# Norm and transpose chains of the output projections set beside the next product

## The chip, the cores and the metric

The kernel runs on one core of a Trainium2 chip. The metric is the device time of one execution in microseconds (us). In the tables PE is TensorE's matmul queue, PEld its weight loads, DVE is VectorE, ACT is ScalarE, POOL is GpSimd and SP is SyncE, which here only issues DMA transfers.

## The reference

One transformer-like block on x of 2048 rows by 1024 columns, in float32:

```python
h = rmsnorm(x, norm_mix_g)
q, k, v, u, vg = split(h @ w_in)                   # five parts of 512 columns
a_out = stick_breaking_attention(q, k, v)          # 8 heads of 64, causal
b_out = spatial_gating(gelu(u), gelu(vg), ...)     # 128-row blocks
mix = concat([rmsnorm(a_out, g[:512]), rmsnorm(b_out, g[512:])])
x = x + mix @ w_out                                # the output projection
h = rmsnorm(x, norm_mlp_g)
x = x + square(relu(h @ w_up)) @ w_down            # 4096 wide
return rmsnorm(x, norm_final_g)
```

## The kernel before, in words

The 2048 rows are worked in four chunks of 512 rows (c = 0 to 3), each of four blocks of 128 rows (tb = 0 to 3). Every float32 operand of a product is split in a high and a low half (`split`: ScalarE copies the high half, L85; VectorE subtracts to get the low half, L86), and each product is three matmuls (`mm3`, L93 to L95).

Attention is a generator, `side`, of 320 weighing steps and 7 more to drain. One step multiplies a query block with 512 keys (`z`, L370 and L371), takes two sigmoids (ScalarE, L377 and L379), a scan and a product (VectorE, L385 and L386), then, for an earlier step's result, four transposes (`tr`, L396), a split (`aT`, L85 and L86) and two matmuls into `av` (L414, L415). A head pair's result goes to DRAM as `a_d` (L426).

The rest of the block is made by other generators. `together(main, side, ratio)` runs `main` and after each of its yields adds `ratio` steps of `side` (0.5 for the output projections of chunks 0 and 1, 0.49 later). For chunks 0, 1 and 2 the order written out is:

1. a loop that runs `side` alone until the chunk's attention is drained;
2. `Out.operands` (5 yields): loads `st` (rows of `b_d`) and `at` (rows of `a_d`); for each tb the norm of `st`, four transposes and a split into `bm`; then the split of `at` into `am`, its squares and 16 column sums on TensorE (L524; 32 matmuls in the trace);
3. `Out.product` (32 yields): four groups, (half, part) = (0,1), (0,0), (1,1), (1,0). Part 1 multiplies `bm`, part 0 `am`. A group is four blocks of 12 matmuls, each added to `ys` on VectorE (L555). After the last group each block is written to `y_d` (L557);
4. `Out.turn` (8 yields): for each tb the norm of the row (squares on ScalarE, L574; `n_r` on GpSimd; scaling on VectorE, L576), and twice four transposes (L581) and a split into `hT`. Chunk 2 keeps no halves and copies `hT` on ScalarE, then writes it to `h_d` (L590).

After chunks 0 and 1 comes `up_plain` (256 yields): 16 rounds that load and split 256 columns of `w_up` (L618) and multiply them with `hT` of both chunks. After chunk 2 comes `down_plain` (256 yields): it loads `ys` of chunks 0 and 1 from `y_d` (L642), then for g = 0 to 7 loads and splits `left` (from `act_d`, L647) and `right` (from `w_down`, L654) and multiplies them, each block added to `ys` by L686.

All tiles of these stages named `t8` (8 KB in each partition) share one pool of 14 buffers; three PSUM banks named `mm` serve products and transposes alike. Tile gives each engine a fixed order of instructions when the program is built: the order of the code is the priority, and an instruction whose operands are not ready by its plan lets a later one go first. All loads and stores of these stages go out on SP's queue, in its fixed order.

Of the kernel before, what the change touches and what calls it, by code (L numbers as in the profile page):

```python
# [12 lines left out]
ALU = mybir.AluOpType  # L13
# [3 lines left out]
P = 128  # L17
D = 1024
# [5 lines left out]
TC = 512  # L24
NTB = TC // P
# [9 lines left out]
def block_kernel(ctx: ExitStack, tc: tile.TileContext, x, x_t, gmix, w_in, ln_g, ln_b, sgw, sgb,  # L35
                 outg, w_out, gmlp, w_up, w_down, gfin, out):
    nc = tc.nc
# [31 lines left out]
    a_d = dram.tile([SBW, T], F32, name="a_d")  # L69
# [262 lines left out]
    steps = [0]  # L332
# [6 lines left out]
    DRAIN = LATE + LAG  # L339
# [148 lines left out]
    class Out:  # L488


        def __init__(self, c, room):
            self.c, self.rm = c, room

        def operands(self):
            rm, c = self.rm, self.c
            self.rbs = []
            self.ready = [self.weights(0, 1)]
            st = rm.t8([4, SBW])
            nc.sync.dma_start(st, b_d[c * TC:(c + 1) * TC, :].rearrange("(n p) d -> p n d", p=P))
            at = rm.t8([4, TC])  # L500
            nc.sync.dma_start(at, a_d[:, c * TC:(c + 1) * TC].rearrange("(n p) t -> p n t", p=P))
            bm = self.bm = rm.pair([4, TC])
            for tb in range(NTB):
                sq = rm.t4([SBW], BF16)
                ssq = rm.small("rb_ssq")
                nc.scalar.activation(sq, st[:, tb, :], AF.Square, accum_out=ssq)
                m = rm.small("rb_m")
                nc.vector.tensor_scalar(m, ssq, 1.0 / SBW, EPS, ALU.mult, ALU.add)
                rb = rm.small("rb", bufs=2 * NTB)
                nc.gpsimd.tensor_tensor(rb, m, mhalf[:, 0:1], ALU.pow)  # L510
                self.rbs.append(rb)
                ps = rm.ps((P, 4, P))
                for e in range(4):
                    nc.tensor.transpose(ps[:, e, :], st[:, tb, e * P:(e + 1) * P], ident)
                ts_ = slice(tb * P, (tb + 1) * P)
                split(bm[0][:, :, ts_], bm[1][:, :, ts_], ps)
                yield
            am = self.am = rm.pair([4, TC])
            split4(am, at)
            nc.scalar.activation(at, at, AF.Square)  # L520
            pssq = rm.ps()
            for tb in range(NTB):
                for e in range(4):
                    nc.tensor.matmul(pssq[:, tb:tb + 1], at[:, e, tb * P:(tb + 1) * P], ones, start=e == 0, stop=e == 3)  # L524
            ra = rsqrt_mean(rm.pool, pssq[:, :NTB], NTB, SBW, "ra")
            self.ras = [ra[:, tb:tb + 1] for tb in range(NTB)]
            yield
# [4 lines left out]
                nc.sync.dma_start(w[i].bitcast(F32), wo_d[half, part, i])  # L532
            return w

        def product(self):
# [7 lines left out]
            ys = self.ys  # L543

            def group(half, part, m, rr):
                ws = self.ready.pop() if self.ready else self.weights(half, part)
                hs = slice(half * 512, (half + 1) * 512)
                for tb in range(NTB):
                    ts_ = slice(tb * P, (tb + 1) * P)
                    ps = rm.ps()  # L550
                    for e in range(4):
                        mm3(ps, m[0][:, e, ts_], m[1][:, e, ts_], ws[0][:, e, :], ws[1][:, e, :], e == 0, e == 3)
                        if e == 1:
                            yield
                    nc.vector.scalar_tensor_tensor(ys[tb][:, hs], ps, rr[tb], ys[tb][:, hs], ALU.mult, ALU.add)  # L555
                    if half == 1 and part == 0:
                        nc.sync.dma_start(y_d[c][:, tb, :], ys[tb])  # L557
                    yield

            yield from group(0, 1, self.bm, self.rbs)  # L560
            yield from group(0, 0, self.am, self.ras)
            yield from group(1, 1, self.bm, self.rbs)
            yield from group(1, 0, self.am, self.ras)

        def turn(self):

# [46 lines left out]
    def up_plain(hTs, rm):  # L613

        for q in range(16):
            acts = rm.t8([2, 2, TC])
            st = rm.t8([2, 8, P])
            nc.sync.dma_start(st, w_up[2 * q:2 * q + 2].rearrange("f p k c -> p f k c"))  # L618
            w = rm.pair([2, 8, P])
            for fi in range(2):  # L620
                split(w[0][:, fi], w[1][:, fi], st[:, fi])
            for fi in range(2):
                for i in range(2):
                    ps = rm.ps()
                    for k in range(KD):
                        h = hTs[i][k // 4]
                        mm3(ps, w[0][:, fi, k, :], w[1][:, fi, k, :], h[0][:, k % 4, :], h[1][:, k % 4, :],
                            k == 0, k == KD - 1)
                        if k % 2 == 1 and k < KD - 1:
                            yield  # L630
                    relu2(acts[:, i, fi, :], ps)
                    yield
            for i in range(2):
                nc.sync.dma_start(act_d[i][:, 2 * q:2 * q + 2, :], acts[:, i])

    def down_plain(rm, placed):

        ys = []
        for c in range(2):
            for t2 in range(2):  # L640
                y = rm.t8([2, D])
                nc.sync.dma_start(y, y_d[c][:, 2 * t2:2 * t2 + 2, :])  # L642
                ys += [y[:, 0, :], y[:, 1, :]]

        def left(c, g):
            st = rm.t8([4, TC])
# [12 lines left out]

        ND = 8  # L660
        c_now, n_now = 0, 0
        for g in range(ND):
            lefts, rights = {}, {}
            for turn in range(4):
                if turn == 2:
                    c_now = 1 - c_now
                elif turn > 0:
                    n_now = 1 - n_now
                c, n = c_now, n_now
                if c not in lefts:  # L670
                    lefts[c] = left(c, g)
                if n not in rights:
                    rights[n] = right(n, g)
                if g == ND - 1 and turn == 2:
                    placed.append(True)
                a, b = lefts[c], rights[n]
                ns = slice(n * 512, (n + 1) * 512)
                for tb in range(NTB):
                    ts_ = slice(tb * P, (tb + 1) * P)
                    ps = rm.ps()  # L680
                    for k in range(4):
                        mm3(ps, a[0][:, k, ts_], a[1][:, k, ts_], b[0][:, k, :], b[1][:, k, :], k == 0, k == 3)
                        if k == 1:
                            yield
                    y = ys[4 * c + tb]
                    nc.vector.tensor_tensor(y[:, ns], ps, y[:, ns], ALU.add)  # L686
                    if g == ND - 1 and turn % 2 == 1:
                        finish(rm, rm.t4([D], BF16), c, tb, y, nc.gpsimd)
                    yield
# [286 lines left out]
    def together(main, side=None, ratio=0.0):  # L976
# [3 lines left out]
        while True:  # L980
# [5 lines left out]
            while due >= 1.0:  # L986
                due -= 1.0
                if next(side, OPEN) is OPEN:
                    return OPEN

    base = ExitStack()
    sp = base.enter_context(tc.tile_pool(name="sp", bufs=1))
    mm_stack = ExitStack()
# [22 lines left out]
    with ExitStack() as es:  # L1016
# [22 lines left out]
        hTs = []  # L1039
        for c in range(2):  # L1040
            while steps[0] < 16 * (c + 1) * (c + 2) + DRAIN:
                next(side)
            o = Out(c, rm)
            together(o.operands(), side, R_O)
            together(o.product(), side, R_O)
            together(o.turn(), side, R_O)
            hTs.append(o.hT)
        together(up_plain(hTs, rm), side, R_U)
        while steps[0] < 16 * 3 * 4 + DRAIN:
            next(side)  # L1050
        o = Out(2, rm)
        together(o.operands(), side, R_U)
        together(o.product(), side, R_U)
        together(o.turn(), side, R_U)
        down = down_plain(rm, placed)
        assert together(down, side, R_U) is OPEN
    with tc.tile_pool(name="ext", bufs=1, side="right", reuse_waits="tile") as ext, \
            tc.tile_pool(name="ps_x2", bufs=5, space=PSUM, reuse_waits="tile") as ps_x2:
# [59 lines left out]
```

## Time and profile before

| | |
|---|---|
| time, median of three runs | 2487.52 us (2482.71 to 2489.91) |
| the profiled execution, its own time | 2484.54 us |
| its span, first to last instruction | 2482.8 us |
| mean granted clock of TensorE | 0.986 of 2.4 GHz |
| busy time of PE, DVE, ACT, POOL | 2423.0, 1684.9, 1202.1, 308.0 us |

The span is what the trace shows; the execution's own time is 1.7 us more, for what lies around it. Busy time is the time in which at least one instruction of an engine ran. A matmul's end is modelled and overlaps the next one's start, so the pace of the matmuls is read from their starts. The granted clock is a mean over a stretch of two levels, 1 (2.4 GHz) and 0.5 (1.2 GHz).

### The profile page before, as it was taken

How to read it: one execution, taken by the hardware profiler on the slowest of the kernel's cores; microseconds unless marked ns; L12 is line 12 of the kernel's file. 1: busy time of each engine (PE TensorE's matmuls, PEld its weight loads, DVE VectorE, ACT ScalarE, POOL GpSimd, SP SyncE). 2: the span in 40 equal slices, each digit the busy share in tenths (PEclk: the TensorE clock that was granted, in tenths of full speed). 3: DMA queues.
4: the chain of work that ended last, by engine and by line, in shares of the span. 5: the costliest groups of instructions: out<-in, count | busy, mean ns of one | idle time of the engine just before them, and what ended most of it. 6: DMA issues, size and time to landing. Idle time of an engine off the chain costs nothing.

```text
span 2482.8 us, 30562 instructions
## 1 busy us (share of the span) xinstructions
PE 2423.0 (98%) x11424; PEld 1986.5 (80%) x11424; DVE 1684.9 (68%) x2276; ACT 1202.1 (48%) x2016; POOL 308.0 (12%) x284
## 2 busy tenths in 40 slices
PE   8999999998899999999999899999999999999998
PEld 7888888886687888888877688888888888888886
DVE  4753678866957666666667878744676655677788
ACT  5443457544636656656655545421244444433334
POOL 1210011000100000000000000000113232214432
PEclk9999999998999999999999899999999999999999
DMA  9788977678544433433474633254524433673422
GB/s 377 298 307 279 317 261 248 194 221 290 190 153 145 123 119 117 124 121 114 127 267 152 200 109 116 92 196 153 204 96 169 150 140 140 245 270 129 170 97 107
DMA packets 161683, 454.99 MB, mean 183 GB/s; under 512 B 13440, under 2 KB 29824, under 8 KB 142080
## 3 DMA queue, kind: packets, MB, share of 16 engines
q1 hardware_dynamic: 150320, 416.34, 49.4%
q0 software_dynamic: 6336, 33.56, 3.3%
q10 hardware_dynamic: 4880, 3.15, 0.4%
q8 instruction: 90, 1.47, 0.2%
q14 instruction: 57, 0.47, 0.1%
HBM read 322.97 MB, written 130.02 MB: 182 GB/s over the span
## 4 chain that ended last, share of the span: by engine, by line
PE 85%; DVE 7%; DMA 4%; issue 2%; ACT 1%; POOL 0%; SPq 0%; POOLq 0%; DVEq 0%; ACTq 0%
PE mm L95 23%; PE mm L94 23%; PE mm L93 23%; PE tr L396 4%; PE av L414 2%; PE z L370 2%; PE av L415 2%; PE z L371 2%; DVE w L86 2%; DMA v_d<-qkv_st 1%; DMA stx<-in_x_t 1%; DMA kt<-k_d 1%; DVE pr L385 1%; PE mm L524 1%; DVE aT L86 1%
## 5 line engine op out<-in xcount | busy, mean ns | idle before, releaser
L93 PE MATMUL mm<-t,t 128*128 128x512 f32 x1280 | 504.6, 396 | 0.0
L95 PE MATMUL mm<-t,t 128*128 128x512 f32 x1280 | 504.6, 394 | 0.0
L94 PE MATMUL mm<-t,t 128*128 128x512 f32 x1280 | 502.9, 393 | 0.0
L377 ACT ACTIVATE kk<-z,rq 128x512 f32<-128x512 f32 (+2 forms) x320 | 201.3, 629 | 289.0 <-PE z L371 176.6
L385 DVE TENSOR_TENSOR_SCAN pr<-kk,pr,zeros 128x513 f32<-128x513 f32 x192 | 246.4, 1284 | 116.9 <-ACT kk L377 116.6
L95 PEld LDWEIGHTS mm<-t,t 128*128 128x128 f32 x1280 | 242.1, 189 | 51.8
L93 PEld LDWEIGHTS mm<-t,t 128*128 128x128 f32 x1280 | 242.7, 190 | 50.6 <-DVE t L86 0.5
L94 PEld LDWEIGHTS mm<-t,t 128*128 128x128 f32 x1280 | 242.7, 190 | 50.1
L85 ACT ACTIVATE aT<-tr 128x512 fp32r<-128x512 f32 (+1 forms) x320 | 172.2, 541 | 97.6 <-PE tr L396 97.0
L86 DVE TENSOR_TENSOR aT<-tr,aT 128x512 fp32r<-128x512 f32 (+1 forms) x320 | 190.9, 599 | 25.8 <-ACT aT L85 25.6
L396 PE MATMUL tr<-ident,b 128*128 128x128 f32 x1088 | 181.5, 280 | 24.2 <-DVE aT L86 22.5
L379 ACT ACTIVATE b<-z,rq 128x512 f32<-128x512 f32 (+2 forms) x320 | 200.7, 628 | 2.8 <-PE tr L396 2.7
L85 ACT ACTIVATE t<-t 128x1024 fp32r<-128x1024 f32 x104 | 104.6, 1059 | 172.7 <-DMA t<-in_w_down 112.1
L396 PEld LDWEIGHTS tr<-ident,b 128*128 128x128 f32 x1088 | 133.8, 143 | 60.3 <-DVE aT L86 30.5
L85 ACT ACTIVATE w<-raw 128x512 fp32r<-128x512 f32 (+1 forms) x135 | 106.8, 802 | 147.7 <-PE mm L95 135.8
L94 PE MATMUL mm<-w,w 128*128 128x512 f32 x448 | 175.1, 391 | 1.3 <-DVE w L86 1.2
L95 PE MATMUL mm<-w,w 128*128 128x512 f32 x448 | 174.6, 390 | 0.0
L382 DVE TENSOR_TENSOR_SCAN pr<-kk,zeros 128x128 f32<-128x128 f32 (+3 forms) x128 | 104.4, 818 | 91.8 <-ACT kk L377 91.5
L86 DVE TENSOR_TENSOR t<-t,t 128x1024 fp32r<-128x1024 f32 x104 | 123.5, 1226 | 39.9 <-ACT t L85 20.1
L95 PE MATMUL mm<-t,w 128*128 128x512 f32 x380 | 150.5, 396 | 0.0
L94 PE MATMUL mm<-t,w 128*128 128x512 f32 x380 | 150.4, 396 | 0.0
L93 PE MATMUL mm<-t,w 128*128 128x512 f32 x380 | 150.4, 396 | 0.0
(229 smaller groups left out, 4745.8 us busy)
## 6 DMA issues: line engine op xcount, KB each, us to landing
w_in<-wi_d SPq DMA_DIRECT2D x40, 1024.0 KB, 8.7
kt<-k_d SPq DMA_DIRECT2D x160, 256.0 KB, 5.0
t<-wo_d SPq DMA_DIRECT2D x32, 1024.0 KB, 9.1
t<-in_w_down SPq DMA_DIRECT2D x28, 1024.0 KB, 7.2
raw<-s_d SPq DMA_DIRECT2D x28, 1024.0 KB, 4.8
wi_d<-w_in POOLq DMA_DIRECT2D x20, 1024.0 KB, 10.7
vt<-v_d SPq DMA_DIRECT2D x80, 256.0 KB, 2.7
t<-in_w_up SPq DMA_DIRECT2D x16, 1024.0 KB, 7.5
```

The source lines that it names most:

```text
L85: nc.scalar.activation(hi, src, AF.Copy)
L86: nc.vector.tensor_tensor(lo, src, hi.bitcast(F32), ALU.subtract)
L93: nc.tensor.matmul(ps, lh, rh, start=first, stop=False, skip_group_check=more)
L94: nc.tensor.matmul(ps, lh, rl, start=False, stop=False, skip_group_check=more)
L95: nc.tensor.matmul(ps, ll, rh, start=False, stop=last, skip_group_check=more)
L370: nc.tensor.matmul(z[:, :Z], ql, kt[:, 0, :Z], start=True, stop=False)
L371: nc.tensor.matmul(z[:, :Z], ql, kt[:, 1, :Z], start=False, stop=not diag)
L377: nc.scalar.activation(kk[:, :L], z[:, :L], AF.Sigmoid, scale=rq[:, 1, row:row + 1])
L379: nc.scalar.activation(b[:, :L], z[:, :L], AF.Sigmoid, scale=rq[:, 0, row:row + 1])
L382: nc.vector.tensor_tensor_scan(pr[:, L - 1::-1], kk[:, L - 1::-1], zeros[:, :L], 1.0, ALU.mult, ALU.add)
L385: nc.vector.tensor_tensor_scan(pr[:, ::-1], kk[:, ::-1], zeros, carry[tb], ALU.mult, ALU.add)
L396: nc.tensor.transpose(tr[:, tb * P:(tb + 1) * P], bs[tb][:, j * P:(j + 1) * P], ident)
```

## The change

`operands` is cut into `operands_b` and `operands_a`, `product` into `load_x` and `group`, and `down_plain` gets a yield behind its first `left` and `right`, ahead of the loads of `ys`. A helper `weave(a, b)` runs two generators turn by turn. The order of chunks 0 to 2 is written out anew:

- chunk 1's `operands_b` (without the load of `at`) is woven into chunk 0's group (1,0);
- chunk 1's group (0,1) is woven into chunk 0's `turn`;
- then chunk 1's attention is drained, `at` loaded, and `operands_a` made; the groups (0,0), (1,1) and (1,0) follow;
- `up_plain` is woven into chunk 1's `turn`, and multiplies a round's two column blocks with chunk 0 before chunk 1;
- for chunk 2, `down_plain` runs to its first yield ahead of group (1,0), and is woven into chunk 2's `turn`.

Chunk 0's and chunk 2's `operands` and all of chunk 3 stay as they were.

```diff
         def operands(self):
+            yield from self.operands_b(True)
+            yield from self.operands_a()
+
+        def operands_b(self, with_a):
...
-            at = rm.t8([4, TC])
-            nc.sync.dma_start(at, a_d[:, c * TC:(c + 1) * TC]...)
+            if with_a:
+                self.load_a()
...
-            for fi in range(2):
-                for i in range(2):
+            for i in range(2):
+                for fi in range(2):
                     ps = rm.ps()
...
     def down_plain(rm, placed):
-        ys = []
-        for c in range(2):
-            for t2 in range(2):
-                y = rm.t8([2, D])
-                nc.sync.dma_start(y, y_d[c][:, 2 * t2:2 * t2 + 2, :])
-                ys += [y[:, 0, :], y[:, 1, :]]
...
+        lefts, rights = {0: left(0, 0)}, {0: right(0, 0)}
+        yield
+        ys = []
+        for c in range(2):
+            for t2 in range(2):
+                y = rm.t8([2, D])
+                nc.sync.dma_start(y, y_d[c][:, 2 * t2:2 * t2 + 2, :])
...
+    def weave(a, b):
+        for _ in a:
+            next(b, None)
+            yield
...
+        def attended(chunks):
+            while steps[0] < 8 * chunks * (chunks + 1) * 2 + DRAIN:
+                next(side)
+        outs = [Out(c, rm) for c in range(3)]
+        attended(1)
+        together(outs[0].operands(), side, R_O)
+        outs[0].load_x()
+        for half, part in ((0, 1), (0, 0), (1, 1)):
+            together(outs[0].group(half, part), side, R_O)
+        ahead = outs[1].operands_b(False)
+        together(weave(outs[0].group(1, 0), ahead), side, R_O)
+        for _ in ahead:
+            pass
+        outs[1].load_x()
+        first = outs[1].group(0, 1)
+        together(weave(outs[0].turn(), first), side, R_O)
+        together(first, side, R_O)
+        attended(2)
+        outs[1].load_a()
+        together(outs[1].operands_a(), side, R_O)
+        for half, part in ((0, 0), (1, 1), (1, 0)):
+            together(outs[1].group(half, part), side, R_O)
+        hTs = [outs[0].hT]
+        up = up_plain(hTs, rm)
+        turned = outs[1].turn()
+        next(turned)
+        hTs.append(outs[1].hT)
+        together(weave(turned, up), side, R_O)
+        together(up, side, R_U)
+        attended(3)
+        o = outs[2]
+        together(o.operands(), side, R_U)
+        o.load_x()
+        for half, part in ((0, 1), (0, 0), (1, 1)):
+            together(o.group(half, part), side, R_U)
         down = down_plain(rm, placed)
+        next(down)
+        together(o.group(1, 0), side, R_U)
+        together(weave(o.turn(), down), side, R_U)
         assert together(down, side, R_U) is OPEN
```

## Rows read from the trace of the kernel before

**Rows 1.** The page's first part: busy us and share of each engine.

```profile
PE 2423.0 (98%) x11424; PEld 1986.5 (80%) x11424; DVE 1684.9 (68%) x2276; ACT 1202.1 (48%) x2016; POOL 308.0 (12%) x284
```

**Rows 2.** Four stretches: length; busy PE, PEld, DVE, ACT, POOL; clock, DMA share, GB/s.

```profile
643.60:693.00 49.40, 36.91 (x195) 28.50 (x195) 47.75 (x72) 38.79 (x76) 5.58 (x7) 0.83 0.73 240
749.20:770.00 20.80, 17.59 (x92) 13.59 (x91) 20.37 (x31) 19.23 (x36) 1.88 (x2) 0.84 0.55 168
1352.20:1395.00 42.80, 31.01 (x155) 22.58 (x153) 39.26 (x52) 31.58 (x58) 2.81 (x3) 0.84 1.01 333
...
1300.00:1352.20 52.20, 52.20 (x260) 43.21 (x259) 37.83 (x53) 22.39 (x42) 2.41 (x3) 1.00 0.33 105
```

**Rows 3.** Timeline of PE, starts: ten matmuls of a product; one attention step.

```profile
640.12 0.39 PE L94 MATMUL mm<-t,t 128*128 128x512 f32 x1
...
642.38 0.40 PE L95 MATMUL mm<-t,t 128*128 128x512 f32 x1
...
743.86 0.39 PE L370 MATMUL z<-kt,qt 128*128 128x512 f32 x1
...
744.32 0.60 PE L396 MATMUL tr<-ident,b 128*128 128x128 f32 x4
744.67 0.47 PE L414 MATMUL av<-aT,vt 128*128 128x512 f32 x1
...
745.22 0.39 PE L93 MATMUL mm<-t,t 128*128 128x512 f32 x1
```

**Rows 4.** VectorE's instructions by line and form, 570 to 1760 us; mean ns behind the comma.

```profile
L385 DVE TENSOR_TENSOR_SCAN pr<-kk,pr,zeros 128x513 f32<-128x513 f32 x166 | 213.0, 1284 | 108.5 <-ACT kk L377 108.2
L86 DVE TENSOR_TENSOR aT<-tr,aT 128x512 fp32r<-128x512 f32 x187 | 126.9, 680 | 17.0 <-ACT aT L85 16.9
L386 DVE TENSOR_TENSOR b<-b,pr 128x512 f32<-128x512 f32 x167 | 114.9, 689 | 11.0 <-DVE pr L385 0.9
L86 DVE TENSOR_TENSOR t<-t,t 128x1024 fp32r<-128x1024 f32 x92 | 108.5, 1219 | 32.5 <-ACT t L85 16.4 <-PE mm L94 15.8
L686 DVE TENSOR_TENSOR t<-mm,t 128x512 f32<-128x512 f32 x93 | 63.3, 685 | 46.5 <-PE mm L95 46.3
L555 DVE SCALAR_TENSOR_TENSOR t<-mm,rb,t 128x512 f32<-128x512 f32 x32 | 24.0, 750 | 54.2 <-PE mm L95 54.2
L576 DVE SCALAR_TENSOR_TENSOR t<-t,n_r,t 128x1024 f32<-128x1024 f32 x16 | 20.6, 1285 | 2.7 <-POOL n_r L79 2.5
```

**Rows 5.** Timelines of SP, ACT and PE: the chain to chunk 1's first product.

```profile
666.55 0.33 SPq L426 DMA_DIRECT2D a_d<-ao  x1
...
669.72 0.55 SPq L501 DMA_DIRECT2D t<-a_d  x1
...
677.70 2.01 ACT L85 ACTIVATE t<-t 128x1024 fp32r<-128x1024 f32 x2 [3.30 <-DMA t<-a_d]
...
688.09 4.83 PE L524 MATMUL mm<-ones,t 128*128 128x1 f32 x32
692.77 0.77 PE L93 MATMUL mm<-t,t 128*128 128x512 f32 x1
```

**Rows 6.** Timelines of SP and PE: first load of `w_up`, first product with it.

```profile
750.07 0.38 SPq L618 DMA_DIRECT2D t<-in_w_up  x1
...
767.35 0.79 PE L93 MATMUL mm<-t,t 128*128 128x512 f32 x1
```

**Rows 7.** Timelines of SP and PE: `h_d`, first load of `w_down`, first product.

```profile
1367.45 4.26 SPq L590 DMA_DIRECT2D h_d<-t  x2
...
1374.16 0.43 SPq L654 DMA_DIRECT2D t<-in_w_down  x1
...
1393.22 0.95 PE L93 MATMUL mm<-t,t 128*128 128x512 f32 x3
```

**Rows 8.** DMA issues, KB each, us to landing: whole page, then 1352.2 to 1395.

```profile
t<-wo_d SPq DMA_DIRECT2D x32, 1024.0 KB, 9.1
...
t<-y_d SPq DMA_DIRECT2D x3, 1024.0 KB, 9.6
```

More of the change, by code (lines that the diff above doesn't have):

```diff
@@ L492, in __init__, with load_a @@
             self.c, self.rm = c, room
+        def load_a(self):
+            self.at = self.rm.t8([4, TC])
+            nc.sync.dma_start(self.at, a_d[:, self.c * TC:(self.c + 1) * TC].rearrange("(n p) t -> p n t", p=P))
         def operands(self):
+            yield from self.operands_b(True)
+            yield from self.operands_a()
+        def operands_b(self, with_a):
             rm, c = self.rm, self.c
@@ L499, in operands @@
             nc.sync.dma_start(st, b_d[c * TC:(c + 1) * TC, :].rearrange("(n p) d -> p n d", p=P))
-            at = rm.t8([4, TC])
-            nc.sync.dma_start(at, a_d[:, c * TC:(c + 1) * TC].rearrange("(n p) t -> p n t", p=P))
+            if with_a:
+                self.load_a()
             bm = self.bm = rm.pair([4, TC])
@@ L517, in operands, with operands_a @@
                 yield
+        def operands_a(self):
+            rm, at = self.rm, self.at
             am = self.am = rm.pair([4, TC])
@@ L533, in weights, with load_x @@
             return w
-        def product(self):
+        def load_x(self):
             rm, c = self.rm, self.c
@@ L542, in product, with group @@
                 self.ys += [y[:, 0, :], y[:, 1, :]]
[L543 to L563, printed above, removed]
+        def group(self, half, part):
+            rm, c, ys = self.rm, self.c, self.ys
+            m, rr = (self.bm, self.rbs) if part else (self.am, self.ras)
+            ws = self.ready.pop() if self.ready else self.weights(half, part)
+            hs = slice(half * 512, (half + 1) * 512)
+            for tb in range(NTB):
+                ts_ = slice(tb * P, (tb + 1) * P)
+                ps = rm.ps()
+                for e in range(4):
+                    mm3(ps, m[0][:, e, ts_], m[1][:, e, ts_], ws[0][:, e, :], ws[1][:, e, :], e == 0, e == 3)
+                    if e == 1:
+                        yield
+                nc.vector.scalar_tensor_tensor(ys[tb][:, hs], ps, rr[tb], ys[tb][:, hs], ALU.mult, ALU.add)
+                if half == 1 and part == 0:
+                    nc.sync.dma_start(y_d[c][:, tb, :], ys[tb])
+                yield
+        def product(self):
+            self.load_x()
+            for half, part in ((0, 1), (0, 0), (1, 1), (1, 0)):
+                yield from self.group(half, part)
         def turn(self):
@@ L661, in down_plain @@
         c_now, n_now = 0, 0
+        lefts, rights = {0: left(0, 0)}, {0: right(0, 0)}
+        yield
+        ys = []
[3 more added lines that the diff above has]
+                nc.sync.dma_start(y, y_d[c][:, 2 * t2:2 * t2 + 2, :])
+                ys += [y[:, 0, :], y[:, 1, :]]
         for g in range(ND):
-            lefts, rights = {}, {}
+            if g > 0:
+                lefts, rights = {}, {}
             for turn in range(4):
@@ L989, in together @@
                     return OPEN
+    def weave(a, b):
+        for _ in a:
+            next(b, None)
+            yield
     base = ExitStack()
@@ L1038, in block_kernel @@
         nc.sync.dma_start(gfin_t, gfin.broadcast_to([P, D]))
-        hTs = []
-        for c in range(2):
-            while steps[0] < 16 * (c + 1) * (c + 2) + DRAIN:
+        def attended(chunks):
+            while steps[0] < 8 * chunks * (chunks + 1) * 2 + DRAIN:
                 next(side)
[L1043 to L1051, printed above, removed]
+        outs = [Out(c, rm) for c in range(3)]
[26 more added lines that the diff above has]
+        o = outs[2]
         together(o.operands(), side, R_U)
-        together(o.product(), side, R_U)
-        together(o.turn(), side, R_U)
+        o.load_x()
+        for half, part in ((0, 1), (0, 0), (1, 1)):
+            together(o.group(half, part), side, R_U)
         down = down_plain(rm, placed)
+        next(down)
+        together(o.group(1, 0), side, R_U)
+        together(weave(o.turn(), down), side, R_U)
         assert together(down, side, R_U) is OPEN
```

## The prediction

> **What bounds the kernel now.** I read the page's engine shares first: PE is busy for 98% of the span [rows 1], so a gain can only come from time in which PE idles or runs at half clock. Next I laid windows along the span to find that time. Where products and attention run together there is none: 1300 to 1352.2 is 52.20 us long, PE is busy for 52.20 and the clock is 1.00 [rows 2]. The stretches that the change touches are the other three of that group. I count as lost the idle time and the share by which the granted clock was short (it has two levels, 2.4 and 1.2 GHz, so a mean of 0.83 is a third of the stretch at half):
>
> - A, chunk 0's `turn` and chunk 1's `operands`, 643.6 to 693: 12.5 idle and 49.4 x 0.17 = 8.4 for the clock, 20.9 us.
> - B, chunk 1's `turn`, 749.2 to 770: 3.2 and 20.8 x 0.16 = 3.3, together 6.5 us.
> - D, chunk 2's `turn` and the start of `down_plain`, 1352.2 to 1395: 11.8 and 42.8 x 0.16 = 6.8, 18.6 us.
>
> That is 46.0 us, the most that the change could win there. The clock fell in each after PE had begun to idle in pieces; B shows what one such fall costs, 3.3 us.
>
> Why PE idles there is in the same rows: DVE is busy for 47.75 of A's 49.40 us, 20.37 of B's 20.80 and 39.26 of D's 42.80, against 37.83 of 52.20 beside products. So A and B are bound by VectorE. D has a second bound: its DMA share is 1.01, at 333 GB/s [rows 2].
>
> **Prices.** Ten matmul starts from 640.12 to 642.38 give 0.226 us each, so a block of 12 is 2.71 us of PE; an attention step is 745.22 - 743.86 = 1.36 us, its four transposes 0.35 of it [rows 3]. On DVE a full step is 1.284 + 0.680 + 0.689 = 2.65 us; a tb of `turn` that keeps halves is 1.285 and two splits of the same operation and shape as `aT`, 0.680 each: 2.65; the evacuation of a block is 0.750 (L555) or 0.685 (L686) [rows 4]. One tb of bare `turn` with one step is thus 5.3 us of DVE against 0.70 + 1.36 = 2.1 of PE: that is the loss. A woven block adds 2.71 to PE and 0.7 to DVE.
>
> **Group (1,0) of chunk 0 with `operands_b`.** Each tb: PE 2.71 + 0.35 + 1.36 = 4.4 us, DVE 0.750 + 0.680 + 2.65 = 4.1. PE stays the bound, so the moved transposes and splits cost their PE time only, as they do now. Their loads (`st`, two weight tiles, two of x) move into a part in which DMA is about as free as in 1300 to 1352.2, share 0.33 [rows 2]. Cover: the product; without it this would be bound by DVE like A.
>
> **A.** With group (0,1) beside `turn`, DVE still has more to do than PE. What comes late next is `am`: its data is known only when attention has drained, and now nothing but attention stands beside that chain. Before, `a_d` is written at 666.55, `at` issued 3.2 us later, its first split comes 8.0 us after that, the column sums 10.4 us after that and take 4.7 to the first product at 692.77: 26.2 us [rows 5]. After, ACT and DVE have no `bm` in this chain. The lower bound is 3.2 + 8.0 + 5.2 (two copies in 2.01, a last subtraction 1.219 [rows 4], squares over as many elements as the copies, taken as 2.0) + 2.4 (the sums at twice the clock) = 18.8; the upper is 26.2. I take 21, nearer the lower, since that work is gone. Until the write, DVE does four evacuations more (3.0) and two `bm` splits fewer (1.4): 22.95 + 1.6 = 24.6 us from 643.6. So A' lasts 24.6 + 21 = 45.6 us. DVE has 45.6 - 10.6 (`turn`) - 3.0 - 2.4 (`am`) = 29.6 us left, 11.2 steps if attention runs ahead. PE's work at full clock is 4 x 3.41 + 2.4 + 11.2 x 1.36 = 31.3, so 14.3 us are lost: a gain of 6.6. With the chain at 18.8 or 26.2 the gain is 7.6 or 4.0. If attention does not run ahead of the 5 steps that the code gives it there, 22.8 are lost, a gain of -1.9.
>
> **B.** The load of `w_up` went out at 750.07 and the first product with it began at 767.35 [rows 6]. Its buffer comes free only when the last group ends (four `hT`, two `ys`, `bm`, `am` and four weight tiles are all 14), and the change leaves that as it is. Only the splits get an earlier place on ACT and DVE. Bounds of the lost time: 3.3 (no idle time, but the clock falls as now) to 8.1 (half such a fall more). I take 5, between 3.3 and the present 6.5: a gain of 1.5. The order chunk 0 before chunk 1 costs nothing: it issues the same matmuls, and covers `hT` with 2 x 24 x 0.226 = 10.8 us.
>
> **D.** Now the operands stand behind `turn`: `h_d`'s writes hold SP's queue from 1367.45, the load of `w_down` follows at 1374.16, and the first product starts at 1393.22 [rows 7], 41 us into the stretch. After, `left` and `right` are loaded and split during groups (1,1) and (1,0). Their splits, 4 x 1.219 = 4.9 us of DVE, have room there: DVE idles for 14.4 of 52.20 [rows 2]. Per woven tb PE has 0.70 + 2.71 + 1.33 (0.98 step) = 4.7 us, and DVE 1.285 + 0.685 + 2.60 = 4.6: PE bound, 19 us in all. Late next is the DMA: four `ys` loads (4.2 MB), `y_d` and `h_d` written (2.1 each), the next `right` (1.05) and the keys of one unit (0.8) are 10.2 MB, at 333 GB/s 30.6 us, 11.6 more than 19. Attention fills 1.36 / 2.65 = 51% of PE in that time, so 5.7 us are lost, and a fall of the clock costs 3.3: 9.0 lost, a gain of 9.6. Bounds: 2 lost (the loads come ahead as in the quiet row) and 15 (11.6 unfilled and 3.3). I take the middle, since part of the `ys` loads can begin during the group.
>
> The Trainium skill's "Perfetto Trace Analysis" (Roofline) bounds the 16 DMA engines at about 435 GB/s together. This stretch shows 333 at a share of 1.01, and the row decides; by the page's figure the 10.2 MB would take an estimated 23.4 us, some 4 us would be short in place of 11.6, and D would gain about 4 us more.
>
> Chunk 0's `operands` and all of chunk 3 are unchanged: nothing. Some ten attention steps (fewer yields run with them) are issued later than before; they come beside `down_plain`, where PE is full either way.
>
> **Sum.** 6.6 + 1.5 + 9.6 = 17.7 us off the profiled execution's 2484.54: 2466.8. Its time stands 3.0 below the median of the runs, 2487.52, so I forecast 2470 us.
>
> **Rivals.** A time within 0.3% (7.5 us) of before can't be told from no change.
>
> *The stall only moves.* Each engine's order is planned, not the code's: A's PE work, 49.4 - 20.9 = 28.5 us, holds 16 steps (28.5 less 6.6 for transposes and sums, by 1.36) where the code issues seven, so the plan already fills holes, and the weaving may do little that it didn't. A without run-ahead gives -1.9, B at its bound -1.6, D at 15 lost +3.6: 0.1, hence 2487. For it speaks DVE's share in A; against it, that no product stood ready in A at all.
>
> *The pool of 14 buffers fills.* In chunk 2's group (1,1) `bm`, `am`, `ys`, its weights (8 tiles) and `left` and `right` with staging (6) are all 14, so the next weights may wait for a buffer; and during `turn` `hT`, `ys`, `left`, `right` and the four new `ys` are 12, the second `right` needs three more. SP issues in order, so such a load also holds the keys of attention behind it, and nothing fills the hole. Price: weights landing in 9.1 us [rows 8]; from the load of `w_down` to its product 19.1 [rows 7]; two falls of the clock, 6.6: 34.8 us, hence 2470 + 35 = 2505. It turns slower than before by more than 0.3% from 25 us on. For it: `h_d` did hold this queue for 4.26 us [rows 7]. Against: buffers of `st` come free after a split, and a group of 4 x (2.71 + 1.33) = 16 us covers 9.1. The skill's "DMA: Bandwidth & Descriptors" (Anatomy of one DMA) says that a semaphore is waited for on the issuing sequencer ahead of dispatch; that agrees with that row.
>
> *More than the sum.* A at 7.6, B at 3.2, D at 16.6: 27.4, hence 2460; without the clock's fall in B 2457. Against it: DVE's sum in A.
>
> **Chances.** The forecast (7.5 to 27 us won, 2460 to 2480) 0.55, more 0.12: faster 0.67. The stall only moves, 0.19: same. The pool fills, 0.14: slower. To leave out two in ten at most, the range goes from 2452 into the pool's case, to 2491.
>
> **What would show it.** Right: in D the first product with `w_down` starts inside chunk 2's transposes, within some 5 us of the last group's end, and the idle PE time there falls to a third; in A group (0,1) lies among chunk 0's transposes, and a hole before the column sums stays, with the clock at half in it; B barely changes. The sum of steady stretches is the same. Wrong: a gap ahead of chunk 2's group (1,0) with PE waiting for `wo_d`, or a hole in A as long as before.

## The result and the profile after

The changed kernel takes 2461.19 us (median of four runs, 2459.22 to 2461.62) against 2485.78 us beside it: a ratio of 0.9898, interval 0.9881 to 0.9916. It is faster by 1.0%. The forecast was 2470 us. One execution of all, of the kernel `d_ys_first` below, took 5333.94 us, over twice as long as the rest, and that kernel's numbers are of its other three.

The profiled execution takes 2460.87 us, 23.7 us less than that of before; its span is 2458.9 us. The first line of the page, to be read against [rows 1]:

```profile
PE 2413.3 (98%) x11424; PEld 1980.0 (81%) x11424; DVE 1683.4 (68%) x2276; ACT 1201.3 (49%) x2016; POOL 311.7 (13%) x284
```

The counts of instructions are those of before, so nothing was saved but waiting and time at half clock. The windows of the three stretches, and a quiet one, columns as in [rows 2]:

```profile
648.80:693.40 44.60, 38.67 (x211) 32.01 (x209) 43.47 (x62) 31.10 (x55) 1.48 (x3) 0.90 0.57 192
734.00:757.00 23.00, 17.74 (x95) 12.87 (x93) 22.50 (x34) 18.35 (x37) 3.77 (x3) 1.00 0.63 193
1325.00:1350.00 25.00, 25.00 (x148) 21.13 (x147) 21.01 (x30) 17.69 (x33) 2.00 (x3) 1.00 1.00 317
1275.00:1325.00 50.00, 50.00 (x236) 41.22 (x235) 35.86 (x47) 20.38 (x34) 1.83 (x2) 1.00 0.48 147
```

Counted as the prediction counts (idle PE and the clock's shortfall):

| stretch | lost before | lost after | gain | forecast |
|---|---|---|---|---|
| A | 20.9 | 5.9 + 4.5 = 10.4 | 10.5 | 6.6 |
| B | 6.5 | 5.3 + 0 = 5.3 | 1.2 | 1.5 |
| D | 18.6 | 0 | 18.6 | 9.6 |

In D the hole is gone: PE is busy for 25.00 of 25.00 us at full clock, with the DMA engines as full as before (share 1.00, 317 GB/s). In A the hole ahead of the column sums is still there. The timelines of SP, ACT and PE along that chain, to be read against [rows 5]:

```profile
672.06 0.33 SPq L426 DMA_DIRECT2D a_d<-ao  x1
...
675.58 0.37 SPq L496 DMA_DIRECT2D t<-a_d  x1
...
681.08 2.00 ACT L85 ACTIVATE t<-t 128x1024 fp32r<-128x1024 f32 x2 [0.46 <-DMA t<-a_d]
...
679.33 0.66 PE L396 MATMUL tr<-ident,b 128*128 128x128 f32 x4 [0.69 <-DVE aT L86]
...
682.03 0.66 PE L396 MATMUL tr<-ident,b 128*128 128x128 f32 x4 [1.69 <-DVE aT L86]
...
684.28 1.12 PE L396 MATMUL tr<-ident,b 128*128 128x128 f32 x4 [1.13 <-DVE aT L86]
...
688.76 4.68 PE L536 MATMUL mm<-ones,t 128*128 128x1 f32 x32
693.31 0.77 PE L93 MATMUL mm<-t,t 128*128 128x512 f32 x1
```

From the write of `a_d` to the first product are 693.31 - 672.06 = 21.25 us. PE has only attention beside it and waits three times for VectorE's `aT`. The clock is at half behind the third of these waits, back at full when the column sums start, and falls again within their 4.68 us (columns as in [rows 2]):

```profile
684.30:687.70 3.40, 3.40 (x11) 2.59 (x12) 3.40 (x5) 2.61 (x4) 0.00 (x0) 0.50 1.00 422
688.76:691.10 2.34, 2.34 (x23) 2.33 (x21) 1.96 (x3) 2.34 (x5) 0.00 (x0) 1.00 0.99 417
691.10:693.31 2.21, 2.21 (x13) 2.21 (x12) 2.21 (x3) 0.13 (x1) 0.00 (x0) 0.50 0.99 235
```

**One count for all kernels.** The measure above counts half-clock time inside a hole (a gap between two matmuls) twice: its gains add up to 30.3 us, and the two executions differ by 23.7. For the comparisons below I add up PE's gaps between its first and its last matmul, and half of the half-clock time outside them, from the trace of each profiled execution. By this count before loses 73.9 us and after 50.3, and the span less that sum is 2405.3 to 2409.4 us in all fourteen kernels, so most of what differs between them is lost time; 4 us of it the count does not place. A is 630 to 710 us of the span, B 720 to 790, C 1230 to 1306 (chunk 2's `operands`, which the change leaves alone), D 1306 to 1420.

| kernel | A | B | C | D | elsewhere | sum |
|---|---|---|---|---|---|---|
| before | 21.2 | 6.2 | 7.3 | 16.2 | 23.0 | 73.9 |
| after | 12.8 | 5.3 | 6.5 | 0.1 | 25.6 | 50.3 |
| a_alone | 13.2 | 8.0 | 12.0 | 16.1 | 24.9 | 74.2 |
| c_phase | 12.6 | 9.6 | 9.3 | 19.0 | 23.0 | 73.5 |
| d_alone | 20.9 | 6.3 | 7.4 | 4.6 | 23.7 | 62.9 |
| without_b | 13.0 | 9.5 | 12.5 | 0.7 | 23.2 | 58.9 |
| d_order_only | 18.7 | 5.1 | 11.6 | 13.2 | 23.5 | 72.1 |
| d_weave_only | 12.8 | 5.5 | 6.5 | 1.0 | 25.9 | 51.7 |
| d_ys_first | 12.7 | 5.2 | 7.2 | 8.3 | 28.3 | 61.7 |
| d_loads_only | 10.1 | 5.5 | 6.5 | 1.8 | 23.6 | 47.5 |
| a_unwoven | 15.2 | 3.8 | 8.5 | 0.5 | 24.3 | 52.3 |
| no_weaves | 13.7 | 4.6 | 11.2 | 6.5 | 27.8 | 63.8 |
| a_drain_early | 6.5 | 5.9 | 8.1 | 1.1 | 26.2 | 47.8 |
| both_best | 6.3 | 6.0 | 7.6 | 3.4 | 25.2 | 48.5 |

Each row is one execution, and medians of one kernel differ by some 2 us from set to set (before: 2485.33, 2486.95 and 2487.63 us in the three sets of experiments). Kernels of different sets are therefore compared by their ratios to before; ratio and medians can differ by 0.1%, and where they do both stand.

### The profile page after: what moved, and what is told of

It reads as the page before. It is cut to its first block, busy times and chain, and to the rows that moved or that the text cites. A ratio compares the mean times of both kernels' runs of the same rounds, so it can differ in the third digit from the quotient of the medians.

```text
span 2458.9 us, 30578 instructions
## 1 busy us (share of the span) xinstructions
PE 2413.3 (98%) x11424; PEld 1980.0 (81%) x11424; DVE 1683.4 (68%) x2276; ACT 1201.3 (49%) x2016; POOL 311.7 (13%) x284
## 4 chain that ended last, share of the span: by engine, by line
PE 83%; DVE 9%; DMA 3%; issue 3%; ACT 1%; POOL 0%; SPq 0%; POOLq 0%; DVEq 0%; ACTq 0%
PE mm L95 23%; PE mm L94 23%; PE mm L93 23%; PE tr L396 4%; PE av L414 2%; PE av L415 2%; PE z L370 2%; PE z L371 2%; DVE w L86 2%; DVE t L86 1%; DVE pr L385 1%; DMA v_d<-qkv_st 1%; PE mm L536 1%; DMA kt<-k_d 1%; DMA w_in<-wi_d 1%
## 5 line engine op out<-in xcount | busy, mean ns | idle before, releaser
L94 PEld LDWEIGHTS mm<-t,t 128*128 128x128 f32 x1280 | 243.1, 190 | 50.3
L86 DVE TENSOR_TENSOR aT<-tr,aT 128x512 fp32r<-128x512 f32 (+1 forms) x320 | 191.2, 600 | 24.6 <-ACT aT L85 24.6
L396 PE MATMUL tr<-ident,b 128*128 128x128 f32 x1088 | 176.2, 275 | 16.6 <-DVE aT L86 15.5
L396 PEld LDWEIGHTS tr<-ident,b 128*128 128x128 f32 x1088 | 132.2, 141 | 49.9 <-DVE aT L86 21.2
L86 DVE TENSOR_TENSOR w<-raw,w 128x512 fp32r<-128x512 f32 (+1 forms) x135 | 151.9, 1127 | 2.5 <-ACT w L85 2.1
L93 PE MATMUL mm<-t,w 128*128 128x512 f32 x380 | 150.3, 396 | 0.8 <-DVE t L831 0.8
L401 POOL CAST aT<-zeros 128x256 fp32r<-128x256 f32 x32 | 29.4, 918 | 957.7 <-PE av L415 803.2
L95 PE MATMUL mm<-t,w 128*128 128x512 f32 x380 | 150.3, 396 | 0.0
```

The source lines that it names most:

```text
L86: nc.vector.tensor_tensor(lo, src, hi.bitcast(F32), ALU.subtract)
L396: nc.tensor.transpose(tr[:, tb * P:(tb + 1) * P], bs[tb][:, j * P:(j + 1) * P], ident)
```

## The experiments

The theory at the start was the prediction's: PE waits in A and D for operands that are formed too late, and what lies beside the turns fills the holes; the parts add up. The rivals: the gain lies in D alone; the weaves do nothing, since each engine's order is planned anyway.

**The parts by themselves** (first set). `a_alone` keeps the cut of `operands`, the early `operands_b(1)` and the weave into chunk 0's turn; `up_plain`, chunk 1's turn, chunk 2 and `down_plain` are as before. `d_alone` keeps the edit of `down_plain` and its calls around chunk 2; the rest is as before. `without_b` takes back the weave into chunk 1's turn and the order in `up_plain`:

```diff
-            for i in range(2):
-                for fi in range(2):
+            for fi in range(2):
+                for i in range(2):
...
-        up = up_plain(hTs, rm)
-        turned = outs[1].turn()
-        next(turned)
-        hTs.append(outs[1].hT)
-        together(weave(turned, up), side, R_O)
-        together(up, side, R_U)
+        together(outs[1].turn(), side, R_O)
+        hTs = [outs[0].hT, outs[1].hT]
+        together(up_plain(hTs, rm), side, R_U)
```

> Only chunk 0's and chunk 1's part of the change (A); the order around up_plain and down_plain is the old one. Theory 1 (each stretch wins by itself what its trace lost): A wins about 10 us, so 2475 to 2477, with about 10 us still lost in A, 6.5 in B and 18.6 in D. Rival (the gain is all in D, A only shifts attention): 2484 to 2487.

Measured: 2483.75 us, ratio 0.9993 (0.9985 to 1.0002). No gain: the theory failed and the rival's time came. But not for the rival's reason: A itself lost 13.2 us in place of 21.2. B lost 1.8 more, C 4.7 more and other places 1.9 more. Of gaps alone, without the clock, A lost 5.9 us less, and B 3.2, C 1.0, D 0.7 and the rest 1.5 us more.

> Only chunk 2's part (D): loads of left and right ahead of group (1,0), down_plain woven into chunk 2's turn. Theory 1: D wins 16 to 18 us, so 2468 to 2470, PE without idle time in chunk 2's turn. Rival (D's gain hangs on the attention steps that A pushes later): less than 10 us, 2476 or more.

Measured: 2472.27 us, 0.9940 (0.9926 to 0.9953): 13 us by the medians and 15 by the ratio, 11.6 of them in D's row, somewhat less than the theory's number and well below the rival's time. In the turn PE still has one hole, of 1.88 us (it ends at 1364.45), with the clock at half behind it; the whole change gains 16.1 us in D.

> The changed kernel with the old order around chunk 1's turn and up_plain (turn first, then up_plain, column block before chunk). Theory 1 (w_up's load comes when the last group ends, in either order): within 2 us of the changed kernel, 2460 to 2463. Rival (the weave there hides the transposes): 4 to 6 us slower, 2465 to 2467.

Measured: 2463.62 us, 0.9908 (0.9893 to 0.9922). Its interval overlaps that of the changed kernel, so what B's edit adds can't be told from nothing. The table has B and C 10 us worse in this execution (2466.37 us, the longest of its four) and other places 2.4 better. Against `d_alone`, which lacks only part A, it is 0.0032 x 2485 = 8 us faster. So A is worth about 8 us once D is there, and by itself nothing that these runs can tell (3.7 us at most, by the interval). Why it keeps its gain beside D and not alone stays open.

**Where A's gain goes.** C's holes differ from kernel to kernel though its code is the same. What differs is the step at which attention stands, by the order of the code, when chunk 2's operands begin: about the 250th before, the 244th in `a_alone` and `without_b`, the 240th after. `c_phase` (third set) is `a_alone` with

```diff
-        together(up_plain(hTs, rm), side, R_U)
+        together(up_plain(hTs, rm), side, 0.5135)
```

> The kernel with the A part alone, and the attention walked a little faster beside the first products of the MLP (0.5135 steps for each part in place of 0.49), so that chunk 2's operands begin at about the 250th step of the attention, as before the change, and not at the 244th. Theory (what A wins is given back because the attention stands at another step when chunk 2's operands and their half clock come): the loss there falls from 12 us to 7 or 8, and the time to 2477 to 2480 us. Rival (the step does not matter, the loss there is that of whichever chain comes last): 2482 to 2485 us.

Timeline of PE, the holes in C, first of `a_alone`:

```profile
1268.84 0.55 PE L396 MATMUL tr<-ident,b 128*128 128x128 f32 x3 [0.32 <-DVE aT L86]
...
1270.95 0.71 PE L370 MATMUL z<-kt,qt 128*128 128x512 f32 x1 [1.33 <-ACT b L379]
...
1274.29 0.69 PE L396 MATMUL tr<-ident,b 128*128 128x128 f32 x2 [2.20 <-DVE aT L86]
...
1277.13 0.48 PE L396 MATMUL tr<-ident,b 128*128 128x128 f32 x1 [1.30 <-DVE aT L86]
```

and of `c_phase`:

```profile
1272.80 0.66 PE L396 MATMUL tr<-ident,b 128*128 128x128 f32 x4 [0.86 <-DVE aT L86]
...
1274.84 0.50 PE L370 MATMUL z<-kt,qt 128*128 128x512 f32 x1 [1.15 <-ACT b L379]
...
1278.05 0.55 PE L396 MATMUL tr<-ident,b 128*128 128x128 f32 x3 [2.22 <-DVE aT L86]
```

and of before:

```profile
1279.64 0.66 PE L396 MATMUL tr<-ident,b 128*128 128x128 f32 x4 [0.86 <-DVE aT L86]
...
1281.68 0.50 PE L370 MATMUL z<-kt,qt 128*128 128x512 f32 x1 [1.16 <-ACT b L379]
...
1284.88 0.90 PE L396 MATMUL tr<-ident,b 128*128 128x128 f32 x3 [2.21 <-DVE aT L86]
```

`without_b` has 0.32, 1.34, 2.60 and 1.30. So the step of attention sets the holes in C: that part of the theory is shown. What the holes cost it does not set. `d_alone` and `d_order_only` (below) begin chunk 2's operands at before's step too and have before's holes to within 0.15 us, and behind these same holes the clock stays at half for 6.8 us in before and `d_alone`, 10.2 in `c_phase` and 17.1 in `d_order_only`, so that C loses 7.3, 7.4, 9.3 and 11.6 us. `a_alone`, with 12.0, also has 17.1 us at half; how much of its loss in C is due to the step stays open. The time, 2481.90 us (0.9982, 0.9974 to 0.9991), is 2.7 us below `a_alone` by the ratios, with overlapping intervals, and lies just under the rival's 2482 to 2485: B and D lost more in this execution. At B too the first holes go with A's edit: 0.7, 0.6 and 1.1 us in before, `d_alone` and `d_order_only`, and 0.1, 0.3 and 1.5 us in `a_alone`, `c_phase` and `without_b`, where attention stands six steps earlier at the same bare turn of chunk 1. No run varied that step alone.

**What did it in D: the call, the order or the weave.** `d_order_only` (third set) is the kernel before with the two loads moved ahead of `ys`, and `down_plain` made where it was, behind the turn. `d_ys_first` (second set) is the changed kernel with the `ys` loads moved back ahead of `left` and `right`, still called ahead of group (1,0). `d_weave_only` (second set) calls `down_plain` behind that group:

```diff
-        down = down_plain(rm, placed)
-        next(down)
         together(o.group(1, 0), side, R_U)
+        down = down_plain(rm, placed)
+        next(down)
         together(weave(o.turn(), down), side, R_U)
```

and `d_loads_only` (first set) calls it early, but weaves nothing:

```diff
-        together(weave(o.turn(), down), side, R_U)
+        together(o.turn(), side, R_U)
```

> The kernel before with one edit: the second stage's first left and right operands are loaded ahead of the four y_d tiles, and nothing is called sooner (down_plain is still made when chunk 2's turn is over). Theory (order and pool: what cost 18 us after chunk 2's turn was 4 MB of y_d standing ahead of 2 MB of operands): most of the 13 us of the D part alone comes by the order, 2471 to 2476 us, and the stall after the turn falls from 16 us lost to under 6. Rival (the loads must be called before group (1,0) to be formed in time): the first right operand still comes late, 2480 to 2485 us, and over 10 us are lost there.

Measured: 2483.12 us, 0.9983 (0.9975 to 0.9992). The theory fell and the rival's time came: the order alone gives 4 us, and D still loses 13.2. SP's timeline of this kernel has the first `left` and `right` go out when the turn is under way (its first transposes start at 1353.22), and PE's has a hole of 4 us behind the turn:

```profile
1354.28 0.60 SPq L654 DMA_DIRECT2D t<-act_d  x1
...
1361.38 0.59 SPq L661 DMA_DIRECT2D t<-in_w_down  x1
...
1375.48 1.11 PE L396 MATMUL tr<-ident,b 128*128 128x128 f32 x4 [4.09 <-DVE aT L86]
...
1378.88 0.95 PE L93 MATMUL mm<-t,t 128*128 128x512 f32 x3
```

The last of these is the first product of `down_plain`, 26 us after the turn's first transposes. In the changed kernel the first block is evacuated 5.6 us after them.

> The changed kernel, but left and right are loaded and split behind group (1,0) in the code, just ahead of the weave. Theory 1 (operands that are there in time are what counts): most of D's 18 us are lost again, 2471 to 2478, with PE idle in chunk 2's turn. Rival (the plan issues the loads early anyway, or attention fills the wait): 2460 to 2464.

Measured: 2460.39 us, 0.9895 (0.9880 to 0.9909), as fast as the changed kernel. SP's timeline shows why: called later by one group, the loads still leave 44 and 30 us ahead of the turn's first transposes (1327.31).

```profile
1283.19 0.32 SPq L654 DMA_DIRECT2D t<-act_d  x1
...
1297.75 0.39 SPq L661 DMA_DIRECT2D t<-in_w_down  x1
```

So it is enough that the call stands ahead of the turn; the plan then finds the place.

> The changed kernel, but the four loads of ys stand ahead of left and right again, all before group (1,0). They take four of the 14 buffers while bm, am, ys and the weights are live. Theory 1 (14 buffers hold the group's tiles and left and right, no more): the weights of group (1,0) or left and right come late, 8 to 20 us slower, 2469 to 2481. Rival (buffers are not short): 2459 to 2463.

Measured: 2471.43 us, 0.9936 (0.9920 to 0.9953), 9 us above the changed kernel by the ratios: the pool's theory holds. SP's timeline:

```profile
1284.87 0.79 SPq L674 DMA_DIRECT2D t<-y_d  x2
...
1299.15 0.49 SPq L654 DMA_DIRECT2D t<-act_d  x1
...
1313.84 0.38 SPq L661 DMA_DIRECT2D t<-in_w_down  x1
...
1321.18 0.53 SPq L544 DMA_DIRECT2D t<-wo_d  x1
...
1327.68 0.32 SPq L544 DMA_DIRECT2D t<-wo_d  x1
```

The weights of group (1,0), which the changed kernel loads at 1297.26, leave 24 and 30 us later: `ys` holds four buffers, and by the view of SP's waits the second of these loads waits 2.7 us for VectorE's split of an operand of `down_plain`, which is when a buffer comes free. PE's timeline shows what that costs, attention alone with holes until the second half lands:

```profile
1317.80 0.63 PE L396 MATMUL tr<-ident,b 128*128 128x128 f32 x4 [1.19 <-DVE aT L86]
...
1321.28 0.55 PE L396 MATMUL tr<-ident,b 128*128 128x128 f32 x3 [1.46 <-DVE aT L86]
...
1323.66 0.66 PE L396 MATMUL tr<-ident,b 128*128 128x128 f32 x4 [1.25 <-DVE aT L86]
...
1327.33 0.44 PE L370 MATMUL z<-kt,qt 128*128 128x384 f32 x1 [1.46 <-ACT b L379]
```

> The changed kernel, but chunk 2's turn is not woven with down_plain; the early loads and splits stay. Theory 1 (products beside the transposes are needed, since the bare turn is bound by VectorE): 5 to 8 us slower than the changed kernel, 2466 to 2469, with PE idle in the turn. Rival (the plan pulls ready products forward itself; the early operands are the whole gain): 2460 to 2463, down_plain's matmuls among the transposes all the same.

Measured: 2457.63 us, 0.9890 (0.9873 to 0.9907). The time lies 2 us under the rival's and far under the theory's, but the rival's mechanism did not come. PE's and DVE's timelines of this kernel show no product inside the turn: its last transposes start at 1335.88, the first block of `down_plain` is evacuated behind them.

```profile
1335.88 1.09 PE L595 MATMUL mm<-ident,t 128*128 128x128 f32 x8 [0.49 <-DVE t L590]
...
1341.10 0.68 DVE L703 TENSOR_TENSOR t<-mm,t 128x512 f32<-128x512 f32 x1
```

From the first to the last start of its transposes the bare turn takes 12.5 us, where the woven one takes 21.8; attention fills it but for three holes of 0.5 to 0.7 us, and the product starts at once behind it since its operands are formed.

**The weaves.** `a_unwoven` (second set) calls chunk 0's turn by itself and then chunk 1's group (0,1); `no_weaves` (third set) does that at all three turns. The early `operands_b(1)`, `left` and `right` stay.

```diff
-        together(weave(outs[0].turn(), first), side, R_O)
+        together(outs[0].turn(), side, R_O)
         together(first, side, R_O)
```

> The changed kernel, but chunk 0's turn runs bare and chunk 1's group (0,1) behind it in the code (operands_b stays early). Theory 1 (priority decides, a bare turn is bound by VectorE): PE idles in the turn again, group (0,1) covers part of the chain to am instead; 0 to 6 us slower, 2461 to 2467. Rival (the plan pulls the ready group forward itself): 2460 to 2462, the group's matmuls among the transposes.

Measured: 2459.18 us, 0.9886 (0.9870 to 0.9903): no difference that can be told. The theory's mechanism came, but not its price: the turn now has holes of 1.34 and 1.66 us, and group (0,1) comes behind it and covers the first part of the chain to `am`.

> The changed kernel with all three weaves of a turn taken out (each turn is called by itself, and the product's first part behind it); chunk 1's operands_b and the first left and right keep their early places. Theory (the plan takes ready products into the holes of a turn by itself, and only what is formed or loaded sooner counts): 2457 to 2464 us, within 3 us of the changed kernel. Rival (each weave is worth some microseconds and the single runs hid it by chance): the holes of three bare turns stay, 2467 to 2473 us.

Measured: 2466.84 us, 0.9926 (0.9914 to 0.9938), at the rival's edge: the three weaves together seem worth 4 us by the medians (24.6 less 20.8 against before) and 7 by the ratios, with intervals that just touch, though neither of the two that were taken out singly was worth any. In the profiled execution (2472.96 us, the longest of its six) D loses 6.5 and C 11.2. The same bare turn of chunk 2 that cost 1.8 us in `d_loads_only` costs 6.5 here (3.4 in holes, the rest by the clock), with attention at another step beside it. So a weave looks worth what attention happens not to fill; that reading rests on these two executions and on `both_best` below, and is not shown.

**A better one.** The chain to `am` starts when attention has drained. `a_drain_early` (second set) runs 0.75 steps for each part of chunk 0's groups in place of 0.5, and drains and loads `at` ahead of chunk 0's turn, so that the turn and group (0,1) stand beside the chain:

```diff
         for half, part in ((0, 1), (0, 0), (1, 1)):
-            together(outs[0].group(half, part), side, R_O)
+            together(outs[0].group(half, part), side, 0.75)
         ahead = outs[1].operands_b(False)
-        together(weave(outs[0].group(1, 0), ahead), side, R_O)
+        together(weave(outs[0].group(1, 0), ahead), side, 0.75)
...
         outs[1].load_x()
+        attended(2)
+        outs[1].load_a()
         first = outs[1].group(0, 1)
         together(weave(outs[0].turn(), first), side, R_O)
         together(first, side, R_O)
-        attended(2)
-        outs[1].load_a()
```

> The changed kernel with 0.75 attention steps in place of 0.5 beside chunk 0's groups, so that chunk 1's attention is drained by group (1,0)'s end, and at is loaded ahead of chunk 0's turn. Theory 1 (what is left of A is the chain from a_d to am): 6 to 10 us faster than the changed kernel, 2451 to 2455, no hole ahead of the column sums. Rival (A is bound by VectorE's work, which only moves): 2458 to 2463.

Measured: 2455.36 us, 0.9871 (0.9856 to 0.9885): 7 us below the changed kernel by medians and ratios alike, with intervals that barely overlap, and the lowest ratio of all, though those of `d_weave_only`, `a_unwoven`, `d_loads_only` and `both_best` overlap it. SP writes `a_d` 15.6 us sooner, and PE has one long hole left in A, of 2.74 us:

```profile
656.51 0.33 SPq L426 DMA_DIRECT2D a_d<-ao  x1
...
659.39 0.37 SPq L496 DMA_DIRECT2D t<-a_d  x1
...
672.81 0.89 PE L396 MATMUL tr<-ident,b 128*128 128x128 f32 x4 [2.74 <-DVE aT L86]
```

A loses 6.5 us in place of 12.8. The column sums start 15.9 us behind that hole, at full clock, and take 3.73 us. `both_best` (third set) adds the bare turn of `d_loads_only`.

> The two edits that took time off the changed kernel together: 0.75 attention steps beside chunk 0's groups, with the wait for chunk 1's attention and the load of a_d ahead of chunk 0's turn; and chunk 2's turn called by itself, with the first left and right still called ahead of group (1,0). If the two add up: 2461 less 6 less 3 is 2452 us, 2450 to 2454. Rival (both gain from the same chance places, falls of the clock at chunk 1's turn and the attention's third run, and do not add): 2455 to 2460 us.

Measured: 2457.36 us, 0.9885 (0.9871 to 0.9900): the two do not add, and the rival's time came. Its reason did not: A keeps its gain (6.3 lost), and D loses 3.4 us without the weave, all of it in holes and none by the clock, which fits `no_weaves`.

## Why the prediction came out as it did

The direction and the range were right; the sum was some 6 us short (17.7 against 23.7 between the profiled executions). The signs that it named came: in D the first product with `w_down` starts among the transposes and no idle time is left, in A group (0,1) lies among chunk 0's transposes and the hole before the column sums stays, and B barely changes. Of the mechanism one half is shown, that operands loaded and formed ahead of a turn end the wait behind it (`d_alone` and `d_loads_only` against `d_order_only`). The other half, that products must stand beside the transposes, does not hold for one turn at a time: `a_unwoven` and `d_loads_only` are as fast without. All three weaves together are worth some 4 to 7 us (`no_weaves`). Step by step:

- **Prices.** Products hold: they start 0.227 us apart (605.18 to 611.98, 30 starts). The chain in A took 21.25 us against the 21 chosen, but that is partly luck, for its terms are 3.5 + 5.5 + 7.7 + 4.5 where the lower bound has 3.2 + 8.0 + 5.2 + 2.4. The last term took 4.7 us for the sums at half clock; they take 3.73 at full clock (`a_drain_early`) and 6.82 at half (`a_unwoven`). A step's price on VectorE was too high: its instructions' spans overlap, and those in A add up to 47.9 us while it is busy for 43.5.
- **A, mis-sized.** 10.5 us for 6.6 (8.4 by the stricter count). The stretch lasts 44.6 us where 45.6 were worked out, and DVE is busy for 43.47 of them, so the bound was right. But PE did 44.6 - 10.4 = 34.2 us of work at full speed in it, not 31.3. Counted in the trace from start to start, with half-clock time halved, the 2.9 us more are attention's (16.6 us where 15.2 stood), the column sums' (3.4 for 2.4) and the products' and transposes' (14.2 for 13.6). For attention each step was priced at the full 2.65 us of DVE; 14 steps, three of them over fewer than 512 keys, found room where 11.2 were worked out.
- **B, right in number, partly by luck.** 1.2 us for 1.5. But idle time grew, from 3.2 to 5.3 us; what was won is the clock's fall, 3.3 us, which the step expected to stay. In `d_weave_only`, with the same code there, the clock does fall, for 3.4 us, and B loses 5.5. The load of `w_up` leaves when the last group ends, as the step said (736.62); its split comes 8.1 us later, and until then PE has attention alone, with holes. Its three timelines:

```profile
736.62 0.46 SPq L632 DMA_DIRECT2D t<-in_w_up  x1
...
744.74 2.01 ACT L85 ACTIVATE t<-t 128x1024 fp32r<-128x1024 f32 x2
...
746.81 0.66 PE L396 MATMUL tr<-ident,b 128*128 128x128 f32 x4 [1.81 <-DVE aT L86]
```

- **D, the step that failed.** 18.6 us for 9.6 (16.1 by the stricter count); the terms that were mis-sized are the wait for the transfers and what attention fills of it. "10.2 MB, at 333 GB/s 30.6 us, 11.6 more than 19" set all the bytes of the stage against 19 us of work, as if all were needed in it. Two things differ. SP's timeline gives the order:

```profile
1265.37 0.33 SPq L654 DMA_DIRECT2D t<-act_d  x1
1282.93 0.39 SPq L661 DMA_DIRECT2D t<-in_w_down  x1
...
1325.27 1.76 SPq L676 DMA_DIRECT2D t<-y_d  x3
...
1332.64 0.59 SPq L661 DMA_DIRECT2D t<-in_w_down  x1
...
1346.77 0.33 SPq L604 DMA_DIRECT2D h_d<-t  x1
```

The writes of `h_d` come behind the next `right`, not ahead of it; 25.00 us at 317 GB/s are 7.9 MB: two of the four writes of `y_d` had left before (1315.47 and 1321.65), and the second of `h_d` leaves behind the window (1350.77). And the woven product is slower than was worked out. DVE's evacuations of the first four blocks:

```profile
1332.33 0.69 DVE L703 TENSOR_TENSOR t<-mm,t 128x512 f32<-128x512 f32 x1 [0.42 <-DMA t<-y_d]
...
1338.54 0.67 DVE L703 TENSOR_TENSOR t<-mm,t 128x512 f32<-128x512 f32 x1
...
1344.59 0.68 DVE L703 TENSOR_TENSOR t<-mm,t 128x512 f32<-128x512 f32 x1
...
1350.49 0.68 DVE L703 TENSOR_TENSOR t<-mm,t 128x512 f32<-128x512 f32 x1
```

They stand 6.1 us apart (18.16 / 3), where 4.7 was the price of a woven tb: the plan runs more attention between them (9.5 us of PE in the window by the trace, where four steps at 1.33 were priced), PE stays full, and the transfers get that time too. The first evacuation waits only 0.42 us for `ys`, and the second `right`, 15.6 us under way, is split at 1348.25, just as the first four blocks end. The bound "2 lost" was nearer than the middle that was taken. The forecast let attention fill 51% of the time that the transfers take beyond the work; in the trace product and attention fill all of the 25 us, and that is what it missed.

- **Group (1,0) with `operands_b`: nothing.** From 600 to 648.8 us PE is busy for 48.59 of 48.80 us, at full clock: one hole of 0.21 us, at 641.81, is all that is lost.
- **The sum adds up only as a whole.** By the stricter count A won 8.4, B 0.9, C 0.8 and D 16.1, and other places lost 2.6: 23.6. Yet A by itself measured nothing, and beside D 8 us. The forecast put the shift of attention at nothing ("PE is full either way"). The runs show that the step sets the holes in C, 2.3 to 5.6 us of gaps in these kernels, and that the clock, which differs behind the same holes, makes 6.5 to 12.5 us lost of them.
- **Rivals.** *The stall only moves* has nearly the time of A alone (2487 for 2483.75), though A's own stall shrank there; it is wrong for the change. *The pool fills* did not happen here, for `left` and `right` go ahead of the 4 MB of `ys`; with the order turned round it did, at 9 us and not 35, since only weights wait and attention goes on. *More than the sum* (2460) is the time that came, mostly through D, as it said (16.6; 16.1 by the stricter count).

## What to carry to other kernels

Look first for what the next product still waits for when a chain of norms ends, and load and form that ahead of the chain, small operands before large late-used tiles; how finely the two are woven in the code mattered less here (nothing that could be told for one weave, some 4 to 7 us for three), where a plan orders each engine. Set against transfer time only the bytes that are queued ahead of the first operand that is needed, and the whole time until it is needed. Where a second stream fills the holes, an edit shifts that stream for all later stages: measure the edit in the whole kernel, and time both with and without its companions.

## What was unexpected in the hardware

In D the transfers' mean is 317 GB/s at a share of 1.00, but single slices go higher. The view of the DMA engines for 1325 to 1350 us, 40 slices of 0.625 us:

```profile
GB/s 0 360 374 249 197 393 236 262 393 433 419 419 433 433 406 380 380 275 413 439 334 426 419 397 387 249 190 170 246 354 374 390 269 151 220 210 305 252 220 213
```

The highest reach 433 to 439. The Trainium skill's "Perfetto Trace Analysis" (Roofline) puts the 16 engines at about 435 GB/s together. These slices agree. The means of 317 GB/s at a share of 1.00 and 333 at 1.01 show that a full share is no proof of the highest rate. A load of 1 MB in this stretch took 15.6 us to land.

The clock is less steady than the waits. Behind three holes in C that are the same in four executions to within 0.15 us, it stayed at half for 6.8, 6.8, 10.2 and 17.1 us, and the loss read there differs by 4.3 us for it.
